# Moving the last gate block of layer a behind its last projections

## The chip, the cores and the metric

The kernel runs on one core of a Trainium2 chip. The metric is the device time of one execution in microseconds. The kernel before took 762.39 us, the median of 3 runs (762.12 to 762.63).

## The reference

Two pre-norm residual layers over x of 256 tokens by 2048 channels, all in float32. Layer a is multi-head latent attention (16 heads), layer b is a block-sparse attention that, at 256 tokens, is plain causal attention with a position bias (16 heads). Cut to layer a, which the change touches:

```python
proj = rms_norm(x, norm_a) @ w_in_a                 # 2048 -> 512 + 256 + 64 + 2048
q_lat, kv_lat, k_rope, gate = split(proj)
q  = rms_norm(q_lat)  @ w_q_up                      # 16 heads x 192
kv = rms_norm(kv_lat) @ w_kv_up                     # 16 heads x (128 + 128)
q, k = per-head norms and rotary part of q and kv, k_rope
o  = softmax(causal(q k^T * scale)) v               # per head
x  = x + (o * silu(gate)) @ w_out_a                 # 2048 -> 2048
```

Layer b then norms x again, projects it to q, k, v and gate, and ends with its own output product.

## The kernel before

Every float32 matrix is split into a high and a low part, and a product is made of three matmuls (high by high, high by low, low by high). Weights stream from memory in pieces of 512 KB at most (`wr`, loaded by SP's queue at line 134). ACT rounds a piece to its high part (`wh`, line 149), DVE subtracts (`wl`, line 150). TensorE's matmuls are chained in the order in which the program emits them (line 193), so TensorE never changes that order.

The work is cut into steps. A step of a gate or output block (`blk_cols`, line 224; 256 output columns) is six matmuls of 256 columns for one 128-row piece of the weights; a block has 16 steps and one PSUM accumulator. A step of a projection (`blk_rows`, line 204) is six matmuls of 384 or 512 columns; it fills two accumulators. Accumulators come from a pool of five PSUM buffers (`ACC`, line 99). The other three PSUM buffers (`pw`, line 100) are the work banks for head scores, head values and transposes.

In layer a there are eight groups of two heads. `group_a(g)` (line 597) gives the main steps of one group: four steps of the q projection and two of the k and v projection, which fill four accumulators. After the last one, `kv_done` (line 611) sums squares on ACT, makes a reciprocal root on DVE (line 296) and reads all four accumulators into `tok` and `rp` (lines 633 to 637). Three transposes follow (`turn`, line 640), each of which is evicted from its work bank by two ACT instructions and one DVE instruction (lines 383, 388, 389). Then each head has three steps (`head_steps`, line 408): s1 makes scores and softmax, s2 flips the attention weights with a DMA transpose on SP's queue (line 405), s3 multiplies by v and by the gate and writes `ogh` and `ogl`, the operands of the output product.

Two lists hold the steps. `main` holds the gate steps, projections and output steps in a fixed order. `side` holds transposes and heads. The planner (`ordered`, line 168) merges them: it takes any side step that is due, and otherwise the next main step. A step is due when those that it needs have ended and their lag, times `SLACK` 1.3, has passed (lags at line 47, in ns: projections to transposes `PA` 9000, transposes to scores `TU` 3000, scores to flip `S1` 4800, flip to values `S2A` 6000), with a limit on work banks. A step listed under `after` must have been placed, with no lag. Line 682 places the last projection step of group g only after s3 of `heads[2 * g - 4:2 * g - 2]`, which for group 7 are heads 10 and 11.

In `main`, the gate block of group g + 1 lies around the projections of group g: its first three steps (`HALF`) ahead of them, the other 13 behind. The eight output blocks (`outs_a`, line 731) come after the last projections; step i of each needs head i. The first four of them are begun with 12 steps each, which need heads 0 to 11 only, and finished after that.

`reload` (line 706), a side step, loads x again (2 MB in four loads) and the mask table of layer b into buffers that layer a used; it is placed when the scores of heads 14 and 15 have been.

Of the kernel before, what the change touches and what calls it, by code (L numbers as in the profile page):

```python
# [34 lines left out]
WARM = 34  # L35
ACC = 5
HALF = 3


NR, NH = 4, 5  # L40
# [52 lines left out]
def trunk(ctx: ExitStack, tc, xT, gains, cst, w_in_a, w_q_up, w_kv_up, w_out_a, w_in_b, w_out_b, outT):  # L93
# [130 lines left out]
    def blk_cols(w, x, done, lag=3000):  # L224

        nk, ns = w.shape[0] // P, w.shape[1] // P
        a = []

        def go(wt, c, k):
            xh, xl = x()  # L230
            if k == 0:
                a.extend(acc("acc") for _ in range(ns // 2))
            for s in range(ns):
                o = a[s // 2][:, (s % 2) * S:(s % 2 + 1) * S]
                ws = slice(s * P, (s + 1) * P)
                first = k == 0 and s % 2 == 0
                last = k == nk - 1
                matmul(o, wt.h[c][:, ws], paired(xh[:, k]), start=first, stop=False)
                matmul(o, wt.h[c][:, ws], paired(xl[:, k]), start=False, stop=False)
                matmul(o, wt.l[c][:, ws], paired(xh[:, k]), start=False, stop=last)  # L240
            if k == nk - 1:
                done(a)

        return _steps(w, go, 3 * ns * 109, lag)
# [85 lines left out]
    def token_scale(ssq, lay, out, needs, more):  # L330


        def f():
            ps = work("ps_st")
            for t in range(2):
                matmul(ps[:, t * P:(t + 1) * P], ssq[:, t * P:(t + 1) * P], ones, start=True, stop=True)
            v = one.tile([P, 2], F32, name="rv_" + lay)
            nc.vector.tensor_scalar(v, ps[:, :2 * P:P], 1.0 / DM, EPS, op0=ALU.mult, op1=ALU.add)
            r = out["r"] = one.tile([P, 2], F32, name="r_" + lay)
            nc.vector.tensor_copy(r, rsqrt(v, 2, "x"))  # L340
            more()

        def g():
            pr = work("ps_r")
            d = wk.tile([P, S], F32, tag="og", name="diag")
            for t in range(2):
                nc.vector.tensor_scalar(d[:, t * P:(t + 1) * P], ident, out["r"][:, t:t + 1], None, op0=ALU.mult)
            matmul(pr[:, :S], ones, paired(d), start=True, stop=True)
            rows = out["rows"] = one.tile([P, S], F32, tag="rr", name="rr_" + lay)
            nc.vector.tensor_copy(rows, pr[:, :S])  # L350

        a = Step(f, 436, 5500, needs, bank=True)
        return a, Step(g, 436, 1500, [a], bank=True)
# [4 lines left out]
    def gate_done(g, rows):  # L358
        def done(a):
            for b in range(len(a)):  # L360
                ub = wk.tile([P, 2, S], F32, tag="gate", name="gate", bufs=4)
                gate_of[g + b] = ub
                x = wk.tile([P, 2, S], F32, tag="gx", name="gx")
                nc.vector.tensor_tensor(x, a[b].rearrange("p (h t) -> p h t", h=2),
                                        rows().unsqueeze(1).to_broadcast([P, 2, S]), op=ALU.mult)
                nc.scalar.activation(ub, x, AF.Tanh, scale=0.5)
                nc.vector.scalar_tensor_tensor(ub, ub, 1.0, x, op0=ALU.add, op1=ALU.mult)
        return done
# [90 lines left out]
    main, side = [], []  # L459
# [129 lines left out]
    gates = [blk_cols(w_in_a[:, LAT + 256 * g:LAT + 256 * (g + 1)], x_a, gate_done(g, rows_a)) for g in range(8)]  # L589
# [106 lines left out]
    for j in range(4):  # L696
        main += [squares[j]] + lat1[2 * j + 2:2 * j + 4]
    main += lat1[10:] + gates[0] + gates[1][:HALF]
    col_a, row_a = token_scale(ssq_a, "a", scale_a, squares, tables)
# [12 lines left out]
    def out_done_a(j):  # L712
        def f(a):
            xt = res["x"]
            c = 2 * j
            both = lines(xt[:, c:c + 2].rearrange("p a b -> p (a b)"))
            nc.vector.tensor_tensor(both, unpaired(a[0]), both, op=ALU.add)
            split_x(c, G_NB)
            split_x(c + 1, G_NB)
            sum_squares(ssq_b, j)  # L720
        return f
# [9 lines left out]
    outs_a = [blk_cols(w_out_a[:, 256 * j:256 * (j + 1)], og, out_done_a(j), 4000) for j in range(8)]  # L731

    for g in range(8):
        main += group_a(g)
        if g == 0:
            kr.after.append(main[-1])
        if g < 7:
            main += gates[g + 1][HALF:] + (gates[g + 2][:HALF] if g < 6 else [])
        gates[g][-1].after.append(row_a)
        if g > 3:  # L740
            gates[g][-1].after += [h[2] for h in heads[2 * g - 8:2 * g - 6]]
# [3 lines left out]
    again = Step(reload, 0, 8000, (), [h[0] for h in heads[14:]] + main[-1:])  # L745
    side.append(again)
    outs_a[0][-1].needs.append(again)
    for b in outs_a[:4]:
        main += b[:12]
    for b in outs_a[:4]:  # L750
        main += b[12:]
    main += sum(outs_a[4:], [])


    x_b = x_a
# [173 lines left out]
```

## Time and profile before

| | us |
|---|---|
| median of 3 runs | 762.39 |
| the profiled execution | 762.7 |
| its span, first to last instruction | 760.9 |
| TensorE busy (PE) | 749.5 |
| weight loads busy (PEld) | 708.8 |
| VectorE busy (DVE) | 599.5 |
| ScalarE busy (ACT) | 521.1 |
| mean granted TensorE clock, as a share of full speed | 0.998 |

Engines are PE (TensorE matmul), PEld (TensorE weight load), DVE, ACT and SP, whose queue issues nearly all DMAs (SPq). Starts are microseconds from the start of the span. A name such as `acc<-ogh,wh` reads output from inputs, by the program's tiles: `acc` is an accumulator, `ps_s`, `ps_o` and `ps_ta` are work banks for scores, values and transposes. In brackets stands how long the engine was idle before the instruction and what ended that. Matmuls overlap, so the distance of two starts is what a matmul costs, not its shown duration.

### The profile page before, as it was taken

The page shows a single profiled execution, that of the slowest core. Times are in us where ns is not written, and L with a number is a line of the kernel's source. Part 1 is how long each engine was busy: PE and PEld are TensorE (multiplying, and loading weights), DVE is VectorE, ACT ScalarE, POOL GpSimd, SP SyncE. Part 2 cuts the span into 40 slices and gives each one's busy share as a digit, 9 for nine tenths or more (in the row PEclk, how much of TensorE's full clock was granted, in tenths as well). Part 3 has the DMA queues.
Part 4 walks back from the last instruction along what each step waited for, and adds up shares of the span by engine and source line. Part 5 has one row for each costly group of instructions (what it writes and reads, how often), then busy time and mean ns, then how long its engine had stood idle before and what let it go on. Part 6 is the DMA issues. An engine that isn't in the chain of part 4 may idle for free.

```text
span 760.9 us, 14905 instructions
## 1 busy us (share of the span) xinstructions
PE 749.5 (99%) x5246; PEld 708.8 (93%) x5246; DVE 599.5 (79%) x1470; ACT 521.1 (68%) x1288; POOL 0.2 (0%) x4
## 2 busy tenths in 40 slices
PE   8999999999999899999999999999999999999997
PEld 8999999999999899998889988998889988899997
DVE  6988899999997696765888877887688957888553
ACT  7877898888877575556667666675677766675442
POOL 0000000000000000000000000000000000000000
PEclk9999999999999999999999999999999999999999
DMA  9875656766657866667777667876778677767761
GB/s 300 241 197 178 174 164 173 196 156 165 170 179 219 249 192 197 193 180 210 224 213 210 203 192 222 241 185 207 188 225 232 190 217 193 224 200 225 255 218 60
DMA packets 137979, 153.24 MB, mean 201 GB/s; under 512 B 47280, under 2 KB 94768, under 8 KB 137904
## 3 DMA queue, kind: packets, MB, share of 16 engines
q1 hardware_dynamic: 137760, 152.27, 69.4%
q8 instruction: 41, 0.67, 0.4%
q14 instruction: 34, 0.28, 0.1%
q10 hardware_dynamic: 144, 0.02, 0.0%
HBM read 139.68 MB, written 2.10 MB: 186 GB/s over the span
## 4 chain that ended last, share of the span: by engine, by line
PE 63%; DMA 2%; DVE 2%; ACT 1%; issue 0%; DVEq 0%; ACTq 0%
PE acc L199 61%; PE ps_o L199 2%; PE ps_s L199 1%; DMA sm<-pz 1%; DMA tok<-flip 1%; DVE wl L150 1%; ACT wh L149 0%; ACT sqa L768 0%; DMA c_sb<-cst 0%; DVE xt L852 0%; DVE tok L774 0%; DVE flip L404 0%; PE ps_r L199 0%; DVE sm L428 0%; DVE sm L421 0%
## 5 line engine op out<-in xcount | busy, mean ns | idle before, releaser
L149 ACT ACTIVATE wh<-wr 128x512 fp32r<-128x512 f32 (+2 forms) x528 | 331.8, 646 | 147.8 <-PE acc L199 132.9
L150 DVE TENSOR_TENSOR wl<-wr,wh 128x512 fp32r<-128x512 f32 (+2 forms) x528 | 346.2, 675 | 88.8 <-ACT wh L149 84.8
L199 PE MATMUL acc<-wh,xh 128*128 128x512 f32 (+1 forms) x448 | 169.1, 377 | 0.8 <-ACT wh L149 0.8
L199 PE MATMUL acc<-wl,xh 128*128 128x512 f32 (+1 forms) x448 | 168.8, 377 | 1.0 <-DVE wl L150 0.9
L199 PE MATMUL acc<-wh,xl 128*128 128x512 f32 (+1 forms) x448 | 167.6, 374 | 0.0
L199 PE MATMUL acc<-ogh,wh 128*128 128x256 f32 x512 | 142.6, 278 | 0.0
L199 PE MATMUL acc<-xh,wh 128*128 128x256 f32 x512 | 142.3, 278 | 0.0
L199 PE MATMUL acc<-xh,wl 128*128 128x256 f32 x512 | 141.3, 276 | 1.0 <-DVE wl L150 0.8
L199 PE MATMUL acc<-ogl,wh 128*128 128x256 f32 x512 | 141.4, 276 | 0.0
L199 PE MATMUL acc<-ogh,wl 128*128 128x256 f32 x512 | 141.3, 276 | 0.0
L199 PE MATMUL acc<-xl,wh 128*128 128x256 f32 x512 | 140.8, 275 | 0.0
L199 PEld LDWEIGHTS acc<-xh,wl 128*128 128x128 f32 x512 | 98.3, 192 | 1.9 <-DVE wl L150 1.9
L199 PEld LDWEIGHTS acc<-ogh,wl 128*128 128x128 f32 x512 | 98.8, 193 | 0.2 <-DVE wl L150 0.2
L199 PEld LDWEIGHTS acc<-ogl,wh 128*128 128x128 f32 x512 | 98.8, 193 | 0.1
L199 PEld LDWEIGHTS acc<-ogh,wh 128*128 128x128 f32 x512 | 98.8, 193 | 0.0
L199 PEld LDWEIGHTS acc<-xl,wh 128*128 128x128 f32 x512 | 98.2, 192 | 0.3
L199 PEld LDWEIGHTS acc<-xh,wh 128*128 128x128 f32 x512 | 98.2, 192 | 0.3
L199 PEld LDWEIGHTS acc<-wl,xh 128*128 128x128 f32 x448 | 84.9, 190 | 14.4 <-DVE wl L150 4.5
L199 PEld LDWEIGHTS acc<-wh,xh 128*128 128x128 f32 x448 | 85.0, 190 | 11.5 <-ACT wh L149 1.4
L199 PEld LDWEIGHTS acc<-wh,xl 128*128 128x128 f32 x448 | 85.0, 190 | 10.1
L199 PE MATMUL acc<-wh,xt 128*128 128x384 f32 (+1 forms) x192 | 57.5, 357 | 0.0
L199 PEld LDWEIGHTS acc<-wh,xt 128*128 128x128 f32 x192 | 35.1, 189 | 1.3
(150 smaller groups left out, 829.5 us busy)
## 6 DMA issues: line engine op xcount, KB each, us to landing
wr<-w_in_b SPq DMA_DIRECT2D x128, 512.0 KB, 4.5
wr<-w_in_a SPq DMA_DIRECT2D x32, 512.0 KB, 4.8
wr<-w_out_a SPq DMA_DIRECT2D x32, 512.0 KB, 4.6
wr<-w_out_b SPq DMA_DIRECT2D x32, 512.0 KB, 4.5
wr<-w_in_a SPq DMA_DIRECT2D x15, 416.0 KB, 5.1
wr<-w_q_up SPq DMA_DIRECT2D x16, 384.0 KB, 3.9
wr<-w_kv_up SPq DMA_DIRECT2D x8, 512.0 KB, 3.7
xt<-xT SPq DMA_DIRECT2D x4, 512.0 KB, 6.5
```

The lines of the kernel that those rows point to most:

```text
L149: nc.scalar.activation(ho, raw, AF.Copy)
L150: nc.vector.tensor_tensor(lo, raw, ho.bitcast(F32), op=ALU.subtract)
L199: chain(nc.tensor.matmul(*args, skip_group_check=True, **kw))
```

## The change

The 16 steps of the last gate block of layer a (`gates[7]`) are taken out of the places around the projections of group 6 and put behind those of group 7. The first ten steps of output block 0 take these places: three behind gate block 6, seven behind the projections of group 6. Behind the projections of group 7 come two more steps of output block 0, then all of gate block 7, then the first 12 steps of output blocks 1 to 4. After that, blocks 0 to 4 are finished, where it was 0 to 3.

```diff
+EARLY = 10
...
-        if g < 7:
-            main += gates[g + 1][HALF:] + (gates[g + 2][:HALF] if g < 6 else [])
+        if g < 5:
+            main += gates[g + 1][HALF:] + gates[g + 2][:HALF]
+        elif g == 5:
+            main += gates[6][HALF:] + outs_a[0][:HALF]
+        elif g == 6:
+            main += outs_a[0][HALF:EARLY]
...
-    for b in outs_a[:4]:
+    main += outs_a[0][EARLY:12] + gates[7]
+    for b in outs_a[1:ACC]:
         main += b[:12]
-    for b in outs_a[:4]:
+    for b in outs_a[:ACC]:
         main += b[12:]
-    main += sum(outs_a[4:], [])
+    main += sum(outs_a[ACC:], [])
```

## Rows read from the trace of the kernel before

**Rows 1.** The page: TensorE busy over the span, and its clock in 40 slices.

```profile
PE 749.5 (99%) x5246; PEld 708.8 (93%) x5246; DVE 599.5 (79%) x1470; ACT 521.1 (68%) x1288; POOL 0.2 (0%) x4
...
PEclk9999999999999999999999999999999999999999
```

**Rows 2.** Waits of PE, 180 to 262: total, times, longest.

```profile
PE ps_o L199 <- ACT ph L436: 2.1, 1, 2.1
PE ps_s L199 <- DVE sr L389: 0.7, 1, 0.7
```

**Rows 3.** Timeline of PE around the values of head 14: start, duration, instruction.

```profile
250.03 0.28 PE L199 MATMUL acc<-ogh,wl 128*128 128x256 f32 x1
252.40 0.38 PE L199 MATMUL ps_o<-ph,vh 128*128 128x256 f32 x1 [2.09 <-ACT ph L436]
...
256.21 0.27 PE L199 MATMUL acc<-ogh,wl 128*128 128x256 f32 x1
```

**Rows 4.** One stretch behind it: length, busy times, granted clock, DMA share, GB/s.

```profile
254.00:255.00 1.00, 1.00 (x7) 1.00 (x7) 0.70 (x2) 0.50 (x1) 0.00 (x0) 0.50 1.07 348
```

**Rows 5.** Timeline of SP's queue: the last loads of x, the last flips.

```profile
242.04 1.48 SPq L710 DMA_DIRECT2D xt<-xT  x3
243.63 5.65 SPq L405 DMA_TRANSPOSE sm<-pz  x2
```

**Rows 6.** Chain of waits that ended last: start, length, what.

```profile
243.63 7.66 DMA sm<-pz
```

**Rows 7.** DMA issues: count, median us from issue to landing.

```profile
sm<-pz SPq DMA_TRANSPOSE x32, 3.4
```

**Rows 8.** One stretch from the end of projection 7, columns as in rows 4.

```profile
214.50:250.10 35.60, 34.91 (x309) 34.67 (x307) 27.64 (x86) 25.70 (x75) 0.00 (x0) 1.00 0.70 198
```

**Rows 9.** Timeline of PE: first matmuls of two output steps in a row.

```profile
238.15 0.27 PE L199 MATMUL acc<-ogh,wh 128*128 128x256 f32 x1
...
238.82 0.28 PE L199 MATMUL acc<-ogh,wh 128*128 128x256 f32 x1
```

**Rows 10.** Timeline of PE at the ends of projections 6 and 7.

```profile
194.41 0.38 PE L199 MATMUL acc<-wh,xt 128*128 128x512 f32 x1
194.62 0.38 PE L199 MATMUL ps_s<-sf 128*128 128x128 f32 x2
...
196.44 0.39 PE L199 MATMUL ps_s<-sf 128*128 128x128 f32 x2
...
214.32 0.38 PE L199 MATMUL acc<-wh,xt 128*128 128x512 f32 x1
```

**Rows 11.** Timeline of DVE: reads of the accumulators of projection 6.

```profile
201.54 0.28 DVE L633 TENSOR_TENSOR rp<-acc,rs_y 128x128 f32<-128x128 f32 x1
201.74 0.74 DVE L636 TENSOR_TENSOR tok<-acc,rs_y 128x256 f32<-128x256 f32 x2
...
202.60 0.75 DVE L636 TENSOR_TENSOR tok<-acc,rs_y 128x256 f32<-128x256 f32 x2
```

**Rows 12.** Timeline of PE: first transpose of group 5.

```profile
185.16 0.60 PE L202 MATMUL ps_ta<-c_sb,tok 128*128 128x128 f32 x4
```

**Rows 13.** Timeline of ACT: its first eviction.

```profile
187.09 0.46 ACT L383 ACTIVATE sf<-ps_ta,gq_a 128x256 f32<-128x256 f32 x1
```

**Rows 14.** Timeline of DVE: last readers of its first two work banks.

```profile
188.30 0.48 DVE L389 SCALAR_TENSOR_TENSOR sr<-ps_ta,gq_a,sr 128x256 fp32r<-128x256 f32 x1
...
189.16 0.75 DVE L389 SCALAR_TENSOR_TENSOR sr<-ps_ta,g_sb,sr 128x512 fp32r<-128x512 f32 x1
```

**Rows 15.** Timeline of DVE: group 7, two root steps and the first accumulator read.

```profile
221.30 0.17 DVE L304 SCALAR_TENSOR_TENSOR rs_t<-rs_t,rs_y 128x12 f32<-128x12 f32 x1
221.51 0.17 DVE L305 SCALAR_TENSOR_TENSOR rs_y<-rs_t,rs_y 128x12 f32<-128x12 f32 x1
...
222.90 0.28 DVE L633 TENSOR_TENSOR rp<-acc,rs_y 128x128 f32<-128x128 f32 x1
```

**Rows 16.** Timeline of PEld: the weight load of head 14's values.

```profile
252.40 0.19 PEld L199 LDWEIGHTS ps_o<-ph,vh 128*128 128x128 f32 x1 [2.28 <-ACT ph L436]
```

## The prediction

> **What bounds the kernel now.** P6 and P7 are the ends of the projections of groups 6 and 7, s1 is a head's scores, s3 its weighted values. I read the page first: TensorE is busy 99% of the span, and its clock is at full speed in every slice [rows 1]. So the time is the matmuls' own time plus the few places where TensorE waits, and the change neither adds nor removes a matmul. A reordering can only move such waits. The next view was the list of what TensorE waited for in the stretch of the change: there are two waits, 2.1 us for the last heads and 0.7 us in front of them [rows 2]. I then read the order of the matmuls there. The weighted values of head 14 start at 252.40, where the matmul before them had started at 250.03 and the next was due 0.11 later, at 250.14: 2.26 us lost [rows 3]. The matmuls behind them run with a granted clock of 0.50 [rows 4], which is 1.2 of the two levels 1.2 and 2.4 GHz, until 256.21: 3.81 us for one head's group and 11 block matmuls that take 0.53 + 0.08 + 11 x 0.112 = 1.85 elsewhere, so 1.95 lost. Together this one place costs 4.2 us; I call it D, and the 0.7 us wait E. What ends D is seen in the SP queue: the last two flips (the DMA transposes of the attention weights) stand behind the reload of x and go out at 243.63 [rows 5], and the chain of waits gives the first one 7.66 us [rows 6] where the median flip takes 3.4 [rows 7].
>
> One more thing in the order: from P7 to this wait TensorE ran 309 matmuls [rows 8], 62 of them transposes and heads, so 247 or 41 output steps (a few records can be missing) of the 48 that need no late head. The planner had put head 14 there by its lags, with some six independent steps still to go. D is not a lack of begun blocks.
>
> **The change part by part.** The accumulators are five PSUM buffers; a projection group takes four, an open gate or output block one.
>
> *Same work.* 16 gate steps leave the place before the projections of group 7 and return after them; 10 steps of output block 0 take it. An output step and a gate step are the same six matmuls: 0.67 us [rows 9]. Both load 512 KB per four steps and split eight columns of weights the same way, so SP's queue, ACT and DVE see the same stream in another order. Cost 0. The fifth block begun early is also order alone: TensorE shows no wait in this stretch besides D and E. Cost 0, and no gain, as D isn't a lack of steps.
>
> *Wait A, the first step of projection 7.* It needs accumulators, and all four others are held by projection 6 until DVE has read them. Before, 13 gate steps and two s1 stand between. Afterwards there are seven output steps: 1.82 for s1 and a step [rows 10], 1.15 for the second s1 and 6 x 0.67, together 7.0 us after P6. DVE's reads of the accumulators begin 6.9 us after P6 (201.54 against 194.62) [rows 10, 11] and the first buffer is free about 0.55 later (201.74 and half of the pair's 0.74), at 7.45; the last at 203.35, which is 8.7. So 0.45 us at the least and 1.7 at the most; the step's second half needs a second buffer, some 0.4 later. I take 0.9, near the low end, since the first half runs meanwhile.
>
> *Wait B, PSUM banks of the transposes.* The last step of projection 7 may only be planned after s3 of heads 10 and 11 (line 682). These are due by the planner 1.3 x (4.8 + 6.0) = 14.0 us after their scores, about 15 and 17 us after P6. Before, projection 7 began 11.3 us after P6 and filled that time. Afterwards it begins near 7 and its five free steps end near 12 to 13; the planner has then nothing to place but the three transposes (due at 1.3 x 9 = 11.7), s3, s3, and only then the last step. On the chip TensorE goes through this without the planner's pauses, but it needs banks: three work banks, taken by the three transposes (0.36 + 0.36 + 0.14 = 0.86 us). The first comes free when ACT and DVE have evicted it. In group 5 that was 188.30 + 0.48 - 185.16 = 3.6 us after the transposes began [rows 12, 14]; bare, from ACT's start to DVE's end, 1.7 [rows 13, 14] and 0.4 for the transposes, 2.1. Minus 0.86: idle for 1.2 to 2.8 us. The second bank comes 1.1 us after the first [rows 14], s3 takes 0.5 of it: 0.6 more. Group 5 has a gate block's end in front of these evictions (0.7 us pieces on ACT and DVE), group 7 has none afterwards, so I take 1.9 + 0.6 = 2.5, between 1.8 and 3.4.
>
> *Wait C, the first gate step after P7.* It opens a block, so it needs an accumulator: output block 0 holds one and projection 7 the other four. Behind it in TensorE's order are 15 gate steps, 48 output steps, and the last heads; none can pass. Ahead of it stand two s1 and the two remaining steps of block 0: 2 x 1.82 = 3.64 us [rows 10]. This is the layout that followed P6, where the first buffer came free at 7.45: 7.45 - 3.64 = 3.8 us idle. From below: ACT's squares and copies (2.3), eleven small operations at 0.2 each [rows 15], a first read (0.55) and 0.4 between engines, 5.5 in all: 1.9. From above: in group 7 before, P7 at 214.54 and the first read at 222.90 [rows 10, 15]; the reads took 1.8 after P6 (201.54 to 203.35), so the last ends near 224.7, 10.2 behind P7: 6.5. I take 3.8, since the softmax of two heads lies in that window as it did after P6.
>
> *Clock after C.* D shows that 2.26 us without a matmul were followed by 1.95 us of loss at half clock [rows 3, 4]. C is longer: I add 1.95. B comes in two pieces, A is below 1 us; the E wait of 0.7 was followed by no such stretch. None for these, up to 1.95 for B in the range.
>
> A rule stands beside this. The weight load of head 14 waited 2.28 us along with its matmul [rows 16]. The Trainium skill ("TensorE: Matmul & The Clock Gate", section "Step-by-step: what each phase is for") says that matmuls stay in program order but that a weight load can be pulled ahead of matmuls in flight. By the rule each of A, B, C would shrink by one load, 0.19 us, 0.6 in all; by the row, nothing. The sum goes by the row.
>
> *E and D.* E came from DVE being late with the third eviction of group 7, behind copies that waited for the flips of heads 12 and 13. Afterwards their scores come some 4 us earlier against the transposes of group 7, as no 12-step run stands before them: -0.7, between -0.7 and 0. D: reload, flips and s3 of heads 14 and 15 are planned by lags counted from the same scores as before, reload first. So the flips stay behind 2 MB of x: I take 0, between -4.2 (gone) and +1.
>
> **Sum.** 0.9 + 2.5 + 3.8 + 1.95 - 0.7 = +8.45. The profiled execution took 762.7 us (span 760.9 and 1.8 around it), 0.3 above the median of 762.39. 762.7 + 8.45 - 0.3 = 770.8.
>
> **The rivals.**
> 1. *Faster: D and E go, and the new waits are small.* With heads 12 and 13 finished before the scores of head 15, DVE reads the mask for head 15 sooner, so the reload behind that read and the flips behind the reload leave sooner. If the flips land 2.3 us earlier, D and its clock loss vanish: -4.9 with E. It decides when A, B and C sum to under 3.4: A 0.2 (one split of 0.69 fewer in its window), B at its bare 1.2 with its second piece covered, C at its bare 1.9, no half clock: 762.4 - 4.9 + 3.3 = 760.8. For it: DVE and ACT get free while TensorE waits. Against it: the reads came 6.9 us after the projection with DVE partly idle, and the flips' place in SP's queue is unchanged.
> 2. *More of the same.* C's buffer is the last one released (8.7 - 3.64 = 5.1) and B also drops the clock: 0.9 + 2.5 + 1.95 + 5.1 + 1.95 = 12.4, E stays: 774.8. For it: 8.36 us to the reads in group 7 before. Against it: that was with ACT behind a late weight load.
> 3. *D goes, the rest as forecast*: 770.8 - 4.2 = 766.6.
> 4. *The gate block finds a buffer* (the change does what its order says, at no cost): A, B at their low ends cancel E and a part of D: about 762.5. Against it: five buffers, five holders.
>
> **How the numbers follow.** About 0.2% (1.5 us) is what a measurement of this kernel tells from no change. Forecast 0.48, rival 2 0.18, rival 3 0.14, rival 4 0.06, rival 1 0.14. Slower by over 0.2%: 0.80; within: 0.06; faster: 0.14. The forecast's own range, with all its terms at one end or the other, is 766 to 779. Rival 1 and the lower half of rival 4 below 762.5 (0.16) and the top of rival 2's terms above 777 (0.04) are left out: 762.5 to 777.
>
> **What would show it.** In TensorE's waits: a new wait of an acc matmul on xh (the gate step) released by DVE's tok line 636, some 4 us, with a clock near 0.5 behind it (C); a wait at the first projection step of group 7 released by the same line (A); a wait of s3 of head 10 or 11 for DVE line 389 (B). D still there, 2 us released by ACT's ph copy. The forecast is wrong if the gate step starts without a wait, if line 636 ends under 5.5 us after P7, or if head 14's flips no longer land late.

## The result and the profile after

The changed kernel takes 768.73 us (median of 6 runs, 767.32 to 772.19) against 762.25 us for the kernel before, measured beside it (6 runs, 760.97 to 763.9). The medians are 6.5 us apart. The ratio is 1.0093, with a 95% interval from 1.0074 to 1.0112, which is 7.1 us. The forecast was 770.8, in a range from 762.5 to 777.

| | before | after |
|---|---|---|
| span of the profiled execution, us | 760.9 | 766.7 |
| TensorE busy, us | 749.5 | 751.0 |
| mean granted clock | 0.998 | 0.996 |
| P6, start of the scores behind projection 6 | 194.62 | 193.91 |
| first matmul of layer b's scale (`ps_st`) | 319.24 | 324.84 |
| P6 to that matmul | 124.62 | 130.93 |

The last line is the one to compare by: it holds as many matmuls of the same shapes in both kernels and grew by 6.31 us. P6 itself lies anywhere between 193.9 and 196.4 in the ten profiles of this study. Up to there all ten issue as many matmuls of the same shapes (in most of the changed kernels three output steps stand for three gate steps), so I don't put a difference ahead of P6 down to the change.

What TensorE waited for in the stretch, in the changed kernel (total, times, longest; lines are one higher than before, by the new constant). These rows answer to [rows 2]:

```profile
PE acc L200 <- DVE tok L637: 2.6, 2, 2.2
PE ps_o L200 <- ACT ph L437: 2.1, 1, 2.1
PE ps_o L200 <- DVE sr L390: 2.1, 1, 2.1
PE ps_o L200 <- DVE og L452: 0.5, 1, 0.5
PE ps_o L200 <- DVE pl L438: 0.2, 1, 0.2
```

The first row is new: accumulators, read by the `tok` instructions. The third and fourth are new as well: work banks. The second is D, still there. The 0.7 us wait E of before is gone. Where each falls is seen in TensorE's timeline (start, duration, instruction, idle time before it and what ended that):

```profile
193.91 0.38 PE L200 MATMUL ps_s<-sf 128*128 128x128 f32 x2
...
201.45 0.40 PE L200 MATMUL acc<-wh,xt 128*128 128x384 f32 x1 [0.38 <-DVE tok L637]
...
207.59 0.38 PE L203 MATMUL ps_ta<-c_sb,ra 128*128 128x128 f32 x2
210.02 0.38 PE L200 MATMUL ps_o<-ph,vh 128*128 128x256 f32 x1 [2.05 <-DVE sr L390]
...
211.68 0.58 PE L200 MATMUL ps_o<-ph,vh 128*128 128x256 f32 x1 [0.52 <-DVE og L452]
...
215.47 0.63 PE L200 MATMUL ps_s<-sf 128*128 128x128 f32 x2
...
219.81 0.28 PE L200 MATMUL acc<-ogh,wl 128*128 128x256 f32 x1
222.32 0.38 PE L200 MATMUL acc<-xh,wh 128*128 128x256 f32 x1 [2.23 <-DVE tok L637]
...
256.08 0.38 PE L200 MATMUL ps_o<-ph,vh 128*128 128x256 f32 x1 [2.08 <-ACT ph L437]
```

201.45 is A, the first step of projection 7. 210.02 and 211.68 are B, the values of heads 10 and 11 behind the transposes. 215.47 is P7, and 222.32 is C, the first gate step. 256.08 is D, head 14.

The granted clock is the column ahead of the last two (stretch, length, busy times, clock, DMA share, GB/s):

```profile
213.00:214.00 1.00, 1.00 (x4) 0.82 (x4) 0.50 (x2) 0.00 (x0) 0.00 (x0) 0.50 0.01 4
...
224.00:225.00 1.00, 1.00 (x12) 1.00 (x11) 1.00 (x4) 0.48 (x1) 0.00 (x0) 1.00 0.00 0
...
257.00:258.00 1.00, 1.00 (x11) 1.00 (x10) 0.91 (x4) 0.71 (x2) 0.00 (x0) 1.00 1.09 351
```

The clock was at half behind B, and at full speed behind C and, unlike before [rows 4], behind D. From 210.02 to 217.43 TensorE ran two heads' values, one projection step and one head's scores, 2 x 0.49 + 1.41 + 1.15 = 3.54 us in the trace of before; it took 7.41, of which 0.52 is the second piece of B. That leaves 3.35. Not all of it is the clock: in experiment 6 the same stretch took 4.55 us with the clock at full, 0.5 more than 3.54 and the second piece, so restarting behind the two waits costs some 0.5. The clock is the other 2.9.

The account of the 6.31 us: A 0.38, B 2.05 + 0.52, C 2.23, the clock and the restarts behind B 3.35, E gone -0.7, D's wait 2.08 + 0.2 where it was 2.1, D's clock loss gone -1.95. The sum is 6.1; it is of this one execution.

### The profile page after: what moved, and what is told of

Its sections match the earlier page's. It is cut to its first block, busy times and chain, and to the rows that moved or that the text cites. A ratio compares the mean times of both kernels' runs of the same rounds, so it can differ in the third digit from the quotient of the medians.

```text
span 766.7 us, 14906 instructions
## 1 busy us (share of the span) xinstructions
PE 751.0 (98%) x5246; PEld 709.2 (93%) x5246; DVE 598.6 (78%) x1470; ACT 521.3 (68%) x1288; POOL 0.2 (0%) x4
## 4 chain that ended last, share of the span: by engine, by line
PE 80%; DVE 8%; ACT 5%; DMA 4%; issue 2%; SPq 0%; ACTq 0%; DVEq 0%
PE acc L200 73%; PE ps_s L200 3%; DVE wl L151 3%; PE ps_o L200 3%; ACT wh L150 2%; DMA tok<-flip 2%; DMA sm<-pz 1%; ACT sqa L774 1%; PE ps_ta L203 1%; DMA wr<-w_in_a 1%; DVE tok L780 1%; DVE tok L637 0%; ACT sqa L608 0%; DVE rs_t L304 0%; DVE rs_t L305 0%
```

## The experiments

The theory: A and C are the wait for the accumulators of the projection ahead, less the steps in between; B is the wait for work banks; D is the flips behind the reload, met by a place in TensorE's order that the planner's lags set. The main rivals: the begun output blocks are the cover that was missing, or the gate block's ACT and DVE work disturbs the last heads. All kernels were timed beside the kernel before; "before" is its median in the same call, and kernels of different calls are best compared by their ratios. The last column is from one profiled execution each, whose own time can lie off the median (765.94 for the first row, 762.29 for "values later").

| kernel | us | before | ratio and interval | P6 to `ps_st` |
|---|---|---|---|---|
| five blocks, gate block unmoved | 762.44 | 761.46 | 1.0011 (0.9997 to 1.0026) | 126.53 |
| changed, 7 early steps | 765.63 | 761.46 | 1.0060 (1.0036 to 1.0084) | 128.18 |
| changed, gate block held open | 766.20 | 761.46 | 1.0063 (1.0040 to 1.0085) | 129.81 |
| changed, transposes later | 766.99 | 761.46 | 1.0071 (1.0049 to 1.0093) | 129.39 |
| before, reload later | 759.04 | 761.91 | 0.9956 (0.9940 to 0.9971) | 121.44 |
| changed, reload later | 765.61 | 761.91 | 1.0049 (1.0034 to 1.0064) | 127.00 |
| before, values later | 764.55 | 761.91 | 1.0033 (1.0017 to 1.0049) | 125.51 |
| five blocks and values later | 758.67 | 761.56 | 0.9958 (0.9944 to 0.9973) | 121.82 |

**1. One part alone: five blocks begun, the gate block unmoved.**

```diff
-    for b in outs_a[:4]:
+    for b in outs_a[:ACC]:
         main += b[:12]
-    for b in outs_a[:4]:
+    for b in outs_a[:ACC]:
         main += b[12:]
-    main += sum(outs_a[4:], [])
+    main += sum(outs_a[ACC:], [])
```

> The kernel before, with five output blocks begun ahead of the last heads instead of four; the gate block stays where it was. Theory (D is set by the planner's lags and the flips behind the reload, not by a lack of begun blocks): no change, within 0.2% of before, TensorE still waits about 2 us for head 14 at the same place in its order. Rival (the begun blocks are the cover): the 2.1 us wait and its half-clock stretch shrink, 2 to 4 us faster.

As the theory had it: the interval holds 1. Head 14 waits as before, and the half clock stays:

```profile
253.16 0.58 PE L199 MATMUL ps_o<-ph,vh 128*128 128x256 f32 x1 [2.39 <-ACT ph L436]
...
254.00:259.00 5.00, 5.00 (x25) 5.00 (x25) 3.14 (x7) 2.52 (x6) 0.00 (x0) 0.50 0.91 289
```

The place of head 14 in the order is set by lags, so more begun steps behind it change nothing.

**2. Steps moved from in front of A's projection to behind it.** In the changed kernel:

```diff
-EARLY = 10
+EARLY = 7
```

> The changed kernel, with 7 instead of 10 steps of output block 0 ahead of the last projections, so 5 instead of 2 behind them. Theory (A and C are both the wait for the accumulators of the projection in front, some 7 us, less the steps that lie between): A grows from 0.4 to about 2.4 us, C falls from 2.2 to about 0.3; time as the changed kernel, 768.7 within 1.5, B unchanged. Rival (C is DVE being late in that place, whatever stands between): C stays near 2 us, A grows all the same, time about 770.7.

```profile
201.87 0.66 PE L200 MATMUL acc<-wh,xt 128*128 128x384 f32 x1 [2.43 <-DVE tok L637]
...
211.91 0.38 PE L200 MATMUL ps_o<-ph,vh 128*128 128x256 f32 x1 [1.97 <-DVE sr L390]
...
222.75 0.38 PE L200 MATMUL acc<-xh,wh 128*128 128x256 f32 x1 [1.60 <-DVE tok L637]
```

A grew by 2.05 us, the three steps' 2.0, as expected. C fell by 0.6 and not by 2.0, so what I expected, 0.3, was far off. I had taken the steps off the 2.2 us measured in the changed kernel; the prediction's own count fits better. P7 lies at 215.33 here, the five steps and two scores end 5.65 later, and the first buffer is free 7.3 after P7 (222.28 and half of 0.75), near the 7.45 of the prediction; 1.7 is left:

```profile
215.33 0.38 PE L200 MATMUL ps_s<-sf 128*128 128x128 f32 x2
```

```profile
222.28 0.75 DVE L637 TENSOR_TENSOR tok<-acc,rs_y 128x256 f32<-128x256 f32 x2
```

The first of these rows is of TensorE, the second of DVE. It is the 6.8 us of the changed kernel that is short (below). The rival, with DVE late whatever stands between, is right in so far as the chain's length moves with what DVE has in between. The time was outside the 768.7 within 1.5 that I expected: from P6 to `ps_st` it is 2.75 us less than in the changed kernel, for reasons neither had. TensorE doesn't wait for head 14 at all, and the half clock lay elsewhere: behind A, where the matmuls from 201.87 to the transposes took 6.81 us and 5.27 in the changed kernel, so 1.5 lost, and not behind B, where it cost 2.9. SP's queue shows why head 14 didn't wait. Here one flip went ahead of the reload:

```profile
241.96 1.22 SPq L406 DMA_TRANSPOSE sm<-pz  x1
243.23 0.57 SPq L711 DMA_DIRECT2D xt<-xT  x1
...
244.39 3.39 SPq L711 DMA_DIRECT2D xt<-xT  x3
247.89 2.05 SPq L406 DMA_TRANSPOSE sm<-pz  x1
```

In the changed kernel all four loads of x precede both flips, as they did before [rows 5]:

```profile
243.78 3.93 SPq L711 DMA_DIRECT2D xt<-xT  x4
247.82 5.15 SPq L406 DMA_TRANSPOSE sm<-pz  x2
```

**3. The gate block itself held open across the last projections.** In the changed kernel:

```diff
         elif g == 5:
-            main += gates[6][HALF:] + outs_a[0][:HALF]
+            main += gates[6][HALF:] + gates[7][:HALF]
         elif g == 6:
-            main += outs_a[0][HALF:EARLY]
+            main += gates[7][HALF:EARLY]
...
-    main += outs_a[0][EARLY:12] + gates[7]
-    for b in outs_a[1:ACC]:
+    main += gates[7][EARLY:]
+    for b in outs_a[:ACC]:
```

> The changed kernel, but the block that is open across the last two projections is gate block 7 itself (3 steps, 7 steps, and its last 6 behind the projections of group 7), and all five output blocks begin after it. Theory: six steps (4.0 us) and two scores (2.3) instead of 3.6 us stand between the projections and the next block that needs an accumulator: C falls from 2.2 to 0.5 to 1 us; A (0.4) and B (2.1 + 0.5) stay, as the order ahead of them is the same: 1.5 us less than the changed kernel, about 767. Rival (it is the gate block's place that costs, through ACT's and DVE's gate work near the last heads): the time goes back to that of before, about 762.

The time is the theory's (766.2), not the rival's. Six steps instead of two stand behind P7, and C is gone, where 0.5 to 1 was expected; the 0.4 us left is A. B and D stay:

```profile
PE ps_o L200 <- DVE sr L390: 2.0, 1, 2.0
PE ps_o L200 <- ACT ph L437: 1.9, 1, 1.9
PE ps_o L200 <- DVE pl L438: 0.8, 1, 0.8
PE ps_o L200 <- DVE og L452: 0.5, 1, 0.5
PE acc L200 <- DVE tok L637: 0.4, 1, 0.4
```

The gate block's own arithmetic again lies near the last heads here, and costs nothing that shows.

**4. The transposes of group 6 behind the values of heads 10 and 11.** In the changed kernel:

```diff
+    for t in turns_of[6]:
+        t.after += [h[2] for h in heads[10:12]]
```

> The changed kernel, with the three transposes of group 6 placed only after the values of heads 10 and 11. Theory (B is the wait for work banks that the transposes hold): the 2.1 us wait for the transposes' eviction in front of head 10 goes; but the two scores then no longer stand ahead of the gate block, its cover falls from 3.6 to 2.2 us, and C grows to about 4 to 5 us: time between 767 and 770. Rival (heads 10 and 11 are late because of their own flips): a wait of about 2 us stays in front of head 10, released by the split or copy of its attention weights.

```profile
208.43 0.38 PE L200 MATMUL ps_o<-pl,vh 128*128 128x256 f32 x1 [0.56 <-DVE pl L438]
...
217.74 0.58 PE L200 MATMUL acc<-xh,wh 128*128 128x256 f32 x1 [4.82 <-DVE tok L637]
```

The wait for the banks went from 2.05 us to none, and head 10 doesn't wait. The 0.56 left is head 11's, for its own weights; the rival had put such a wait at 2 us, for head 10. C grew to 4.8, inside the 4 to 5 expected from a cover of 2.2 us. The time, 767.0, is at the low end of what was expected. So B is the banks. Removing it moves the waiting to C, because the two scores need the transposes and no longer stand ahead of the gate step; behind this longer wait the clock was at 0.50 from 217 to 223.

**5. The reload of x placed behind the flips of heads 14 and 15, in the kernel before.**

```diff
-    again = Step(reload, 0, 8000, (), [h[0] for h in heads[14:]] + main[-1:])
+    again = Step(reload, 0, 8000, (), [h[1] for h in heads[14:]] + main[-1:])
```

> The kernel before, with the reload of x placed after the flips of heads 14 and 15 are issued in the program, not after their scores. In SP's queue the flip of head 14 then stands ahead of three of the four loads of x, and that of head 15 ahead of two. Theory (D is the flips behind the reload): the 2.1 us wait for head 14 and the half clock behind it go, 3 to 4 us faster than before, about 758. Rival (D is the planner's place for head 14 and a flip that is slow anyway): the wait stays near 2 us, the time within 0.2% of before.

Measured 2.9 us faster than before in the same call, somewhat under the 3 to 4 expected. The chain of waits gives the first flip 5.48 us, where it was 7.66 [rows 6]; the median flip takes 3.5 here, so the flip is still slow, but in time. SP's queue, and TensorE at head 14, now without a wait:

```profile
242.38 1.22 SPq L405 DMA_TRANSPOSE sm<-pz  x1
...
244.44 0.47 SPq L710 DMA_DIRECT2D xt<-xT  x1
245.32 1.61 SPq L405 DMA_TRANSPOSE sm<-pz  x1
...
252.38 0.28 PE L199 MATMUL ps_o<-ph,vh 128*128 128x256 f32 x1
```

TensorE's order at this place is as before, so this shows D's cause: the flips' place behind the loads of x.

**6. The same edit in the changed kernel.**

> The changed kernel with the same later reload. Theory: D goes here too, 2.3 us of wait and at times the half clock behind it, 2 to 4 us less than the changed kernel, 765 to 767; the waits A, B and C stay at 0.4, 2.1 + 0.5 and 2.2, so it stays slower than before by 3 to 5 us. Rival (the change's loss sits in the last heads): the time returns to that of before.

D is gone, A, B and C stay, and the kernel is still 0.49% slower than before, as the theory had it. The waits that remain are A, B (its second piece, 0.52, is not shown) and C:

```profile
203.99 0.40 PE L200 MATMUL acc<-wh,xt 128*128 128x384 f32 x1 [0.39 <-DVE tok L637]
...
212.48 0.38 PE L200 MATMUL ps_o<-ph,vh 128*128 128x256 f32 x1 [1.97 <-DVE sr L390]
...
215.88 0.38 PE L200 MATMUL ps_s<-sf 128*128 128x128 f32 x2
...
217.03 0.27 PE L200 MATMUL acc<-ogh,wh 128*128 128x256 f32 x1
...
219.41 0.28 PE L200 MATMUL acc<-ogh,wl 128*128 128x256 f32 x1
222.08 0.49 PE L200 MATMUL acc<-xh,wh 128*128 128x256 f32 x1 [2.39 <-DVE tok L637]
```

From 212.48 to 217.03 is the stretch behind B that took 7.41 us in the changed kernel; here it took 4.55, at full clock. The half clock lay behind C this time (last section). DVE's first reads of the accumulators into `tok`:

```profile
221.61 0.75 DVE L637 TENSOR_TENSOR tok<-acc,rs_y 128x256 f32<-128x256 f32 x2
```

With D away from both kernels the change costs 765.61 - 759.04 = 6.6 us.

**7. Head 14 and 15's values planned later, in the kernel before.**

```diff
+    for h in heads[14:]:
+        h[1].lag = 9000
```

> The kernel before, with the values of heads 14 and 15 planned 3.9 us later (their flips' lag 9000 instead of 6000), so that some six more of the begun output steps stand ahead of head 14; SP's queue keeps its order. Theory: there were six independent steps left, the flips land 2.3 us too late, so the wait at head 14 goes and with it the half clock: about 758, 3 to 4 us faster, and the flip still takes some 7 us. Rival (the begun blocks were used up): TensorE waits as long, at a later place, and the time stays.

A miss: 0.33% slower, where 3 to 4 us faster was expected. Head 14 no longer waits, but two output steps behind it do:

```profile
253.12 0.28 PE L199 MATMUL ps_o<-ph,vh 128*128 128x256 f32 x1
...
257.98 0.38 PE L199 MATMUL acc<-ogh,wh 128*128 128x256 f32 x1 [1.47 <-ACT ogh L452]
...
260.62 0.38 PE L199 MATMUL acc<-ogh,wh 128*128 128x256 f32 x1 [1.36 <-ACT ogh L452]
```

The six steps that I had counted as free stood between the values of the last heads and the output steps that read them, and covered the gate product and the split. Used ahead of head 14, they are missing behind it.

**8. Five blocks begun and the values later, together, in the kernel before** (the edits of 1 and 7).

> The kernel before, with five output blocks begun and the values of heads 14 and 15 planned 3.9 us later. The later values alone moved the wait: head 14 no longer waited, but the begun steps ran out behind it and two output steps waited 1.5 and 1.4 us for ogh of heads 14 and 15. Theory: the fifth block's 12 steps then lie between the values and their readers, no wait of 1 us or more is left between the scores of head 15 and the end of the begun blocks, 3 to 4 us faster than before, about 758. Rival (order and begun blocks don't matter, the flips set the end): a wait of 2 us or more stays in that stretch, the time is within 0.3% of before.

2.9 us faster than before, just under the 3 to 4 expected. In the whole stretch TensorE waits only for this:

```profile
PE ps_s L199 <- DVE sr L389: 0.7, 1, 0.7
PE acc L199 <- DVE wl L150: 0.4, 2, 0.2
```

So the fifth block has a worth, but only once the planner places the last heads late enough to use it; alone it is worth nothing (1), and the place alone costs (7). This kernel and that of 5 beat both kernels of the case, by the same amount, since in both head 14 no longer waits: in 5 the flips land in time, here the begun steps cover them.

## Why the prediction was right, step by step

**Same work, and no gain in the fifth block.** Held (experiment 1), but my reason was half right: experiment 7 shows that the six steps left over at head 14 were not spare.

**A**, put at 0.9: 0.38 measured. The step started 7.5 us after P6 (201.45 - 193.91), when the first buffer was free, as read from projection 6 before [rows 10, 11]. The 0.45 added for the step's second half was wrong: it did not wait.

**B**, put at 1.9 + 0.6: 2.05 + 0.52. The first piece is the bank of the first transpose, released by the row that answers to [rows 14]; experiment 4 confirms it. The second piece has the right size and the wrong cause: head 11 waited for DVE's read of head 10's values (line 452), so it took head 10's bank and not that of the second transpose.

**C**, put at 3.8: 2.23. The mechanism held (experiments 2, 3, 4); the size was off, because the chain that reads the accumulators was shorter than 7.45. Experiment 6 shows it best, with the clock at full ahead of C: the steps ahead took the forecast's 3.64 us (215.88 to 219.52), but the first buffer was free 6.1 us after P7 (221.61 and half of 0.75). In the changed kernel the first of the steps ahead ran at half clock, and both were longer by nearly as much: the steps took 4.4 (215.47 to 219.9), and the buffer was free after 6.8:

```profile
221.64 0.29 DVE L634 TENSOR_TENSOR rp<-acc,rs_y 128x128 f32<-128x128 f32 x1
221.85 0.74 DVE L637 TENSOR_TENSOR tok<-acc,rs_y 128x256 f32<-128x256 f32 x2
```

What the forecast took over from P6 was not the same work: DVE had one weight split (`wl`) in this window, in the changed kernel and in experiment 6, where two lay behind P6 before and three in experiment 2, in which the buffer took 7.3. One split went with 6.1 and 6.8 us, two or three with 7.3 to 7.5; no run varies them alone, so that they make the difference is not shown.

**The clock**, put at 1.95 behind C, and at nothing, or 1.95 at the most, behind B: 2.9 behind B, or 3.35 with the restarts, and nothing behind C. This term was mis-sized and misplaced in the profiled execution, and it is also why D, whose wait stayed, cost 1.95 less there than before. It is not settled by the order of the steps: in experiment 6 the same waits left the clock at full behind B and at half behind C, as forecast. The six runs of the changed kernel, of 767.32 to 772.19 us, had mean clocks from 0.998 to 0.992.

**The sum** came out near, 6.1 against 8.45. The forecast was too high by 1.6 in C and by 0.5 in A. Its three errors of the clock, 3.35 too little behind B, 1.95 too much behind C and 1.95 not taken off behind D, nearly cancelled. That is luck: no row told where the half clock would lie.

**The weight loads.** The rule of the Trainium skill ("TensorE: Matmul & The Clock Gate", "Step-by-step: what each phase is for"), by which a load may be pulled ahead, gave nothing here: at C the load stood idle 2.42 us and started with its matmul.

```profile
222.31 0.19 PEld L200 LDWEIGHTS acc<-xh,wh 128*128 128x128 f32 x1 [2.42 <-DVE tok L637]
```

**E and D.** E went as said. D's wait stayed at 2.1 us as said, by the order of SP's queue; it is no fixed property of the change, as experiment 2 lost it by a different order in that queue. The forecast's own range, 766 to 779, leaves out D's low end of -4.2, which stands as rival 3 instead.

**The rivals.** The faster one needed D to go and A, B, C to stay under 3.4 us together. D stayed, and the three came to 5.2. Even with D removed from both, the change loses (6). "More of the same" was right that B drops the clock, but needed C at the last buffer, 5.1, and it ended at the first. "D goes, the rest as forecast", at 766.6, is as near to the measured 768.73 as the forecast's 770.8: the time doesn't tell the two apart, the trace does, as D's wait is there. "The gate block finds a buffer" is out by C's wait.

## What to carry to other kernels

A step that opens a new accumulator right behind the step that filled the last ones waits for the chain of work that ends in the first read of those, 6.1 to 7.5 us here, so at least that much other work has to stand between; before, 13 steps did, afterwards two to seven. Work begun early covers a late result only if the order has it both ahead of the result and between the result and its readers. Before moving work to cover a wait, look at what makes the result late: here 2 MB of loads stood in one queue ahead of two flips, and moving the loads gave 2.9 us.

## What was not expected of the hardware

Waits of nearly the same length did and did not cost the clock. Behind 2.05 us (changed kernel, B) it was 0.50 in the stretch shown; behind 1.97 us at the same place in experiment 6 it was 1.00 from 212 to 217; behind C it stayed at 1.00 after 2.23 us in the changed kernel, and in experiment 6, after 2.39, it was 0.66 over five us (0.50 from 223 to 225). The two rows of experiment 6, around B and behind C:

```profile
212.00:217.00 5.00, 4.00 (x26) 3.60 (x27) 3.15 (x9) 3.81 (x20) 0.00 (x0) 1.00 0.59 200
222.00:227.00 5.00, 4.92 (x29) 4.93 (x30) 4.61 (x15) 1.07 (x3) 0.00 (x0) 0.66 0.17 33
```

What decides it stays open; a forecast of this kernel should take a wait of two microseconds with and without some 2 to 3 us of clock loss on top (1.95 behind D before, 2.9 behind B).
